# One head of 96 loaded in an order whose outermost count is 8 (softmax times V, one core)

## Chip, core, metric

One core of a Trainium2 chip. The time is what the device takes for one execution, in microseconds (us); lower is better. Quoted times are medians. Ratios are the mean time of one kernel's fast runs over that of the other's fast runs of the same rounds, so they are not quite the ratios of the medians. "More than before" in the experiments is the difference of the two medians of one call. DRAM is the memory off the core that holds the inputs and SBUF the memory on the core with 128 partitions into which loads write.

## The reference

```python
scores: (8, 12, 1024, 1024) float32, v: (8, 12, 1024, 64) float32
attn = np.exp(scores - scores_max)
attn = attn / (np.sum(attn, axis=-1, keepdims=True) + 1e-8)
return np.matmul(attn, v).astype(np.float32)
```

That is 96 heads. Each reads 4 MB of scores and 256 KB of v, and writes 256 KB.

## The kernel before

What matters is how a head is brought in. A head is a tile of 128 partitions; partition p takes 8 adjacent rows of scores, 32 KB in one piece. From here on, a row is such a 32 KB piece. All transfers go through one queue in a fixed order, and the load of head n+4 is asked for when head n is nearly done. (Cuts are marked with `# ...`.)

```python
AHEAD = 4
sc_bh  = scores.rearrange("b h (p r) j -> (b h) p r j", p=P)
v_bh   = v.rearrange("b h (p c) d -> (b h) p c d", p=P)
out_bh = out.rearrange("b h (p r) d -> (b h) p r d", p=P)
# ...
def load(n):
    v_sb = v_pool.tile([P, C, D], FP32, tag="v_sb", name="v_sb")
    queue(nc.sync.dma_start(out=v_sb[:], in_=v_bh[n]))
    s_nat = s_pool.tile([P, R, SK], FP32, tag="s_nat", name="s_nat")
    step = EB if n == BH - 1 else R
    for r in range(0, R, step):
        queue(
            nc.sync.dma_start(out=s_nat[:, r : r + step, :], in_=sc_bh[n, :, r : r + step, :])
        )
    loaded[n] = (s_nat, v_sb)
# ... per head: exp on ACT, transposes on PE, copies on DVE, matmuls with v, then
    if r == R - 1:
        queue(nc.sync.dma_start(out=out_bh[n], in_=st["out_sb"][:]))
# ...
        if r == R - 1 and n + AHEAD < BH:
            load(n + AHEAD)
```

The softmax here doesn't subtract the row's maximum and nothing guards it: scores larger than these inputs give would overflow.

## Time and profile before

| | before |
|---|---|
| time | 1089.68 us |
| one head, from issue to issue | 11.01 us |
| busiest compute engine in 11 us | PE, 8.15 us |
| a 32 KB scores row on one DMA engine, median | 1.216 us |
| transfers of the one queue, share of 16 DMA engines | 98.5% |

Here, in addition, is the page's rate of transfer in 40 equal slices of the span (27 us each), and the rate in two stretches in the middle, in the order stretch, length, busy time of PE, weight loads, DVE, ACT and POOL with their instructions, then clock, DMA share and GB/s.

```profile
GB/s 396 423 430 425 423 423 427 427 426 428 427 422 423 424 431 427 422 426 424 431 425 429 425 426 424 425 429 428 424 423 430 424 426 427 428 420 428 426 398 160
```

```profile
529.00:540.00 11.00, 8.02 (x128) 7.53 (x128) 6.56 (x13) 7.31 (x5) 0.62 (x1) 0.84 1.01 427
540.00:551.00 11.00, 7.87 (x128) 7.49 (x128) 6.55 (x13) 7.30 (x5) 0.62 (x1) 0.83 1.01 427
```

From the second slice to the last but two the rate stays between 420 and 431, and 427 GB/s is about 16 times the 27 GB/s of one engine (32 KB in 1.216 us). Nearly the whole time of the kernel is this one number.

One thing about the sixteen engines is in no view and comes from the trace's completion records, sixteen per load. The completions of one load lie 0.6 us apart at the start of the kernel, 1.9 us at 35 us, and 10.4 us in the middle (for head 47: first 528.25, last 538.63). The engines drift apart until some are nearly a head ahead of others, and by the last full load the spread is 20 us. The trace has a candidate for what drives them apart. Beside the loads it shows packets of 16 KB on a queue of their own (count, MB, share of 16 engines):

```profile
q8 instruction: 96, 1.57, 0.6%
```

They come about once per head and last 1.07 us. Likewise about once per head one engine falls back: the delays of the sixteen behind the first one add up to 1.6 us more with each head (median). That fits, but no run tests it.

The packet records name the queue and not the engine. Where the text below says "all engines", it means that no fast row, or next to none, is left in that stretch.

### The profile page before, as it was taken

The page shows a single profiled execution, that of the slowest core. Times are in us where ns is not written, and L with a number is a line of the kernel's source. Part 1 is how long each engine was busy: PE and PEld are TensorE (multiplying, and loading weights), DVE is VectorE, ACT ScalarE, POOL GpSimd, SP SyncE. Part 2 cuts the span into 40 slices and gives each one's busy share as a digit, 9 for nine tenths or more (in the row PEclk, how much of TensorE's full clock was granted, in tenths as well). Part 3 has the DMA queues.
Part 4 walks back from the last instruction along what each step waited for, and adds up shares of the span by engine and source line. Part 5 has one row for each costly group of instructions (what it writes and reads, how often), then busy time and mean ns, then how long its engine had stood idle before and what let it go on. Part 6 is the DMA issues. An engine that isn't in the chain of part 4 may idle for free.

```text
span 1088.4 us, 27687 instructions
## 1 busy us (share of the span) xinstructions
PE 782.8 (72%) x12288; PEld 743.7 (68%) x12288; DVE 628.2 (58%) x1156; ACT 704.0 (65%) x385; POOL 60.1 (6%) x102
## 2 busy tenths in 40 slices
PE   3767777676777767677776767777676777767676
PEld 3667667676766767677676767677676767767676
DVE  2556556565555655556565655655565565556555
ACT  4667576666757666665766666575665757566675
POOL 0000000000000000000000000000000000000000
PEclk9888878778787877878888887878888787787888
DMA  9999999999999999999999999999999999999994
GB/s 396 423 430 425 423 423 427 427 426 428 427 422 423 424 431 427 422 426 424 431 425 429 425 426 424 425 429 428 424 423 430 424 426 427 428 420 428 426 398 160
DMA packets 42024, 454.77 MB, mean 418 GB/s; under 512 B 4656, under 2 KB 4656, under 8 KB 29232
## 3 DMA queue, kind: packets, MB, share of 16 engines
q1 hardware_dynamic: 41904, 453.00, 98.5%
q8 instruction: 96, 1.57, 0.6%
q14 instruction: 24, 0.20, 0.0%
HBM read 427.82 MB, written 25.17 MB: 416 GB/s over the span
## 4 chain that ended last, share of the span: by engine, by line
DMA 96%; DVE 1%; PE 1%; issue 0%; SPq 0%; ACT 0%; DVEq 0%; ACTq 0%
DMA out_dram<-out_sb 69%; DMA s_nat<-in_scores_dram 18%; DMA v_sb<-in_v_dram 9%; DVE out_sb L89 1%; PE psT L140 1%; PE psO L77 0%; SPq L120 0%; ACT p_nat L136 0%; DVE pt L146 0%; SPq L115 0%; DVE recip L88 0%; DVEq L89 0%; SPq L96 0%; ACTq L136 0%
## 5 line engine op out<-in xcount | busy, mean ns | idle before, releaser
L136 ACT ACTIVATE p_nat<-s_nat 128x2048 f16<-128x2048 f32 x384 | 702.8, 1901 | 375.8 <-DMA s_nat<-in_scores_dram 364.7
L140 PE MATMUL psT<-ident,p_nat 128*128 128x128 f16 x6144 | 621.6, 264 | 274.5 <-ACT p_nat L136 273.5
L140 PEld LDWEIGHTS <-p_nat 128*128 128x128 f16 x6144 | 524.9, 155 | 301.5 <-ACT p_nat L136 295.2
L146 DVE COPY pt<-psT 128x1024 f16<-128x1024 f16 x768 | 529.0, 691 | 307.2 <-PE psT L140 285.4
L77 PE MATMUL psO<-vones,pt 128*128 128x65 f16 x6144 | 343.0, 204 | 27.3 <-DVE pt L146 26.3
L77 PEld LDWEIGHTS <-pt 128*128 128x128 f16 x6144 | 295.4, 107 | 39.2 <-DVE pt L146 38.3
L89 DVE TENSOR_TENSOR out_sb<-psO,recip 128x256 f32<-128x256 f32 x192 | 73.6, 420 | 98.7 <-DMA out_dram<-out_sb 98.6
L130 POOL CAST vones<-v_sb 128x512 f16<-128x512 f32 x96 | 59.4, 619 | 1007.3 <-DMA v_sb<-in_v_dram 995.5
L88 DVE RECIPROCAL recip<-psO 128x4 f32<-128x4 f32 x192 | 34.1, 178 | 49.9 <-PE psO L77 49.9
L136 ACT ACT_TABLE_LOAD x1 | 1.3, 1283 | 0.7 <-PEq L168 0.7
L64 DVE MEMSET vones<- 128x8 f16 x3 | 0.1, 65 | 0.8 <-PEq L168 0.8
L58 DVE CAST ident<-ident 128x128 f16<-128x128 f32 x1 | 0.2, 227 | 0.4 <-POOL ident masks.py:199 0.4
masks.py:199 POOL TENSOR_SCALAR_AFFINE_SELECT ident<-ident 128x128 f32<-128x128 f32 x1 | 0.3, 294 | 0.1
masks.py:197 POOL MEMSET ident<- 128x128 f32 x1 | 0.2, 205 | 0.3 <-POOLq L168 0.3
L168 POOL MEMSET const-float32-0.0<- 128x1 f32 x1 | 0.1, 99 | 0.2 <-issue 0.2
L168 POOL MEMSET const-bfloat16-1.0<- 128x1 bf16 x1 | 0.1, 102 | 0.0
L168 POOL MEMSET const-uint8-127<- 128x1 uint8 x1 | 0.1, 102 | 0.0
L168 POOL MEMSET const-float32-1.0<- 128x1 f32 x1 | 0.1, 99 | 0.0
## 6 DMA issues: line engine op xcount, KB each, us to landing
s_nat<-in_scores_dram SPq DMA_DIRECT2D x95, 4096.0 KB, 32.5
v_sb<-in_v_dram SPq DMA_DIRECT2D x96, 256.0 KB, 23.5
out_dram<-out_sb SPq DMA_DIRECT2D x96, 256.0 KB, 32.4
s_nat<-in_scores_dram SPq DMA_DIRECT2D x4, 1024.0 KB, 23.8
```

What stands on the lines that cost most here:

```text
L58: nc.vector.tensor_copy(out=ident16[:], in_=ident32[:])
L64: nc.vector.memset(vo[:, :, D : D + 1], 1.0)
L77: nc.tensor.matmul(out=psO[:, g, :], lhsT=pt[:, c * P : (c + 1) * P], rhs=st["vones"][:, c, :], start=(c == 0), stop=(c == C - 1),)
L88: nc.vector.reciprocal(out=recip[:], in_=psO[:, :, D : D + 1])
L89: nc.vector.tensor_tensor(out=st["out_sb"][:, r - G + 1 : r + 1, :], in0=psO[:, :, 0:D], in1=recip[:].to_broadcast([P, G, D]), op=mybir.Al ...
L130: nc.gpsimd.tensor_copy(out=vones[:, :, 0:D], in_=v_sb[:])
L136: nc.scalar.activation(out=p_nat[:], in_=s_nat[:, r : r + EB, :], func=EXP)
L140: nc.tensor.transpose(out=psT[:, c * P : (c + 1) * P], in_=p_row[:, c, :], identity=ident16[:],)
L146: nc.vector.tensor_copy(out=pt[:], in_=psT[:])
L168: nc = _bacc.Bacc("TRN2", target_bir_lowering=False, num_devices=1)
```

## The change

The intent is to let eight engines instead of sixteen carry one head in the middle, by giving the load an outermost count of 8. Memory rows then land in permuted partitions, and the output store of that head undoes the permutation.

```diff
         if r == R - 1:
-            queue(nc.sync.dma_start(out=out_bh[n], in_=st["out_sb"][:]))
+            dst = out_bh[n]
+            if n == BH // 2:
+                dst = dst.rearrange("(b a) r d -> a b r d", a=8)
+            queue(nc.sync.dma_start(out=dst, in_=st["out_sb"][:]))
 ...
         step = EB if n == BH - 1 else R
+        if n == BH // 2:
+            queue(
+                nc.sync.dma_start(
+                    out=s_nat[:],
+                    in_=sc_bh[n].rearrange("(b a) r j -> a b r j", a=8),
+                )
+            )
+            loaded[n] = (s_nat, v_sb)
+            return
```

## The prediction

> **What bounds the kernel now.** I first read the page's opening lines, for which engine is full, and then its chain of waits, for what the end hangs on.
>
> ```profile
> PE 782.8 (72%) x12288; PEld 743.7 (68%) x12288; DVE 628.2 (58%) x1156; ACT 704.0 (65%) x385; POOL 60.1 (6%) x102
> DMA  9999999999999999999999999999999999999994
> ...
> q1 hardware_dynamic: 41904, 453.00, 98.5%
> ...
> DMA 96%; DVE 1%; PE 1%; issue 0%; SPq 0%; ACT 0%; DVEq 0%; ACTq 0%
> ```
>
> No compute engine is busy for over 72%. The transfers of one queue take 98.5% of what 16 DMA engines have, in every slice but the last, and 96% of the chain is DMA. The kernel is a stream of heads through the DMA engines. Next I read the issue queue in a quiet stretch, for the rhythm of one head and for how far ahead the kernel asks, and then its waits.
>
> ```profile
> 516.68 0.33 SPq L115 DMA_DIRECT2D v_sb<-in_v_dram  x1
> 517.38 0.33 SPq L120 DMA_DIRECT2D s_nat<-in_scores_dram  x1
> 518.19 0.34 SPq L96 DMA_DIRECT2D out_dram<-out_sb  x1
> 527.69 0.33 SPq L115 DMA_DIRECT2D v_sb<-in_v_dram  x1
> ...
> SPq L115 <- DMA s_nat<-in_scores_dram: 803.6, 89, 10.4
> ...
> s_nat<-in_scores_dram SPq DMA_DIRECT2D x95, 4096.0 KB, 32.5
> ```
>
> One head takes 527.69 - 516.68 = 11.01 us. A scores load lands 32.5 us after its issue, which is three heads. The queue's main wait, in front of the next v load, is for a scores load to land. The built program says which one: there are eight completion semaphores, and each issue waits for the one issued eight before it. Counting v, scores, out, v, ..., the v load of head k waits for the scores of head k-3. So about three heads are in flight, and the four buffers are not the limit.
>
> The trace's packet records give the rate of one engine. A scores row is one packet of 32768 bytes, median 1.216 us, which is 27 GB/s; a v or output row is one of 2048 bytes, 0.084 us. Each of 16 engines has 8 rows of each kind per head: 8 x 1.216 + 16 x 0.084 = 11.07 us, against a period of 11.01. So every engine is full without a gap, and whatever one engine is given in addition has to be paid at the end, unless it is made up by idle time that does not exist. Compute has room:
>
> ```profile
> 513.00:524.00 11.00, 8.15 (x139) 7.77 (x137) 6.58 (x13) 7.31 (x5) 0.62 (x1) 0.84 1.01 427
> ```
>
> The columns are PE, weight loads, DVE, ACT, POOL, clock, DMA share and GB/s: the busiest engine works 8.15 us of 11.00. So compute does not make a late head later; it only moves with it.
>
> [...]
>
> **The change, part by part.** Nothing is added to any compute engine, and the order of instructions on the queue stays the same; the other 95 heads are untouched. The permutation is undone by the output store, so the result is right. What changes is head 48's 128 rows: sixteen per engine on engines 0 to 7, none on 8 to 15.
>
> Step 1, engine time. Engines 0 to 7 carry 8 extra rows of 32 KB: 8 x 1.216 = 9.73 us; and 8 extra output rows: 8 x 0.084 = 0.67 us. Together 10.4 us.
>
> Step 2, who pays. [...]all later heads are again split evenly over 16. Engines 0 to 7 are full before and after, so they never make up the 10.4 us; the other eight run ahead and idle later. Head 48 lands on the loaded eight 1.3 + 19.5 = 20.8 us after head 47 (v and out first). Until then the others have heads 49 and 50 in their rings, 2 x 11.0 + 1.3 = 23.3 us of work, so they don't even run dry. This step alone makes 1089.7 + 10.4 = 1100.1 us.
>
> Step 3, [...]Engines are not in step, though. The 2 KB packets around one head start between about 503.0 and 507.5 us[...]. When head 48 takes over 23 us, engines 8 to 15 run dry because the issue of head 51 waits for head 48; that idle time is the lead they have anyway, and costs nothing more.
>
> [...]0.55 x 31 + 0.2 x 20 + 0.25 x 10.4 = 24 us. As the middle of the distribution lies on the strong side, I say 26: 1089.7 + 26 = 1116 us.
>
> **Rivals.** (a) Engine time alone, 1100 us: speaks for it that 27 GB/s is seen as an engine's rate[...].[...] (b) It hides: engines 8 to 15 run ahead, head 48 is late but something absorbs it, about 1090 us. For it: compute has 2.8 us of room per head, and three heads are in flight. Against: the full engines are DMA's own, and depth moves no work from one engine to another. I give it 0.04. (c) The late head starves compute, and compute becomes the bound behind it. PE needs 8.15 us per head and gets 11, so each wait is recovered within the next heads; adds nothing. (d) The DRAM side is read in steps of 256 KB[...] and is slower for it; the trace has no such pattern, and I can't size it, but it only adds.
>
> **Range and chances.** Rival (a) sets the lower edge, 1099; the strong form without much skew the upper one, 1131. The line at 2% is 1111.5 us, which the strong form passes and (a) does not: slower 0.56, same 0.43, faster 0.01.
>
> **What would show it.** If step 1 and 2 hold, all of the loss is between the landing of head 47 and of head 48 (about 530 to 590 us), and the heads after that follow at 11.0 us again. If step 3 holds, the packets of 32 KB in that stretch last 2.4 to 3.6 us instead of 1.216, on even the engines that don't carry head 48, and the DMA rate falls below 400 GB/s there while engines are busy. [...]It is wrong altogether if the load is still split over 16 (no change), or if engines differ between load and store (0.7 us less).

The sum. The grounds of step 3, a model of where each engine writes and of how engines slow each other there, are cut. In its strong form, step 1's 10.4 us included, it came to 28 to 33 us more than before. The sum weighs three cases: the strong form as 31 us with 0.55, a weaker one as 20 us with 0.2, and step 1 alone, 10.4 us, with 0.25. It came to 24 us, raised to 26, so 1116 us. Only 10.4 was worked out from the trace before; what 31 and 20 are made of, no trace showed then. The sign against step 3: all packets at 1.22 us, head 48 about 21 us after head 47, and 427 GB/s until the end. The 2.4 to 3.6 us for step 3 are two and three times 1.216, an estimate of the model.

The engines. "Engines 0 to 7" and "8 to 15" are names for the eight that carry head 48 and the eight that don't; no record numbers them. The trace after bears the number out: the changed load has eight engine completions where a plain load has sixteen, and the page counts 4640 packets under 512 B against 4656 before (16 for each of the 291 transfers), eight fewer for the load and eight for the store.

The waits. That an issue waits for the one eight before it is in the trace before: the landings name eight semaphores, and the v load issued at 538.69 us follows the landing, at 538.63, of the scores load issued at 506.37, eight issues earlier.

## The result, and the profile after

1128.4 us (four runs, 1125.91 to 1129.83) against 1089.68: ratio 1.0352, 95% interval 1.0331 to 1.0373, slower. The time lies in the predicted range, 12 us above the predicted 1116. The profiled run is the fastest of the four; its span is 1124.1 us against 1088.4, so the profile has 35.7 of the 38.7 us to show.

The page's rate of transfer after, 28 us to a slice:

```profile
GB/s 401 424 425 423 428 423 428 426 424 426 426 427 425 425 426 426 426 424 404 214 260 407 429 404 423 427 423 430 422 427 426 427 421 425 424 428 424 424 388 90
```

Two slices at about half the rate, and a last one of 90 in place of 160. The rest is as before. The stretches of the middle, same columns as above:

```profile
511.00:522.00 11.00, 7.85 (x128) 7.48 (x125) 6.55 (x12) 7.31 (x5) 0.62 (x1) 0.78 1.01 424
529.00:540.00 11.00, 8.01 (x128) 7.62 (x128) 5.71 (x10) 5.56 (x4) 0.19 (x1) 0.84 1.08 248
540.00:551.00 11.00, 2.43 (x22) 2.31 (x23) 1.91 (x4) 4.39 (x3) 0.62 (x1) 0.55 1.01 223
551.00:562.00 11.00, 6.62 (x109) 6.37 (x106) 4.65 (x9) 2.93 (x2) 0.00 (x0) 0.81 1.01 215
562.00:573.00 11.00, 0.00 (x0) 0.00 (x0) 0.00 (x0) 0.00 (x0) 0.00 (x0) 0.50 1.07 229
573.00:584.00 11.00, 0.00 (x0) 0.00 (x0) 0.00 (x0) 0.00 (x0) 0.00 (x0) 0.50 0.77 245
584.00:595.00 11.00, 7.05 (x101) 6.93 (x102) 5.37 (x10) 7.32 (x4) 0.62 (x1) 0.62 0.91 378
```

Read the last two columns together. From 529 to 573 the DMA share is 1.0, all sixteen engines have a packet in flight all the time, and yet they move 215 to 248 GB/s instead of 427. So this is not idle engines: every engine is slow. The packet records say the same: between 531 and 576 us the kernel before has 516 rows of 32 KB, 513 of them under 1.3 us; the kernel after has 267, and not one under 2.2 us (median 2.47). As no fast row is left, the engines that carry nothing of head 48 are among the slow ones. Only between 573 and 584 are some engines idle as well (0.77).

The issue queue and its longest wait, and ACT (start, length, what, and in brackets how long ACT had been idle and for what):

```profile
516.89 0.79 SPq L123 DMA_DIRECT2D s_nat<-in_scores_dram  x1
546.57 0.33 SPq L118 DMA_DIRECT2D v_sb<-in_v_dram  x1
585.94 0.33 SPq L118 DMA_DIRECT2D v_sb<-in_v_dram  x1
596.55 0.33 SPq L118 DMA_DIRECT2D v_sb<-in_v_dram  x1
```

```profile
SPq L118 <- DMA s_nat<-in_scores_dram: 828.8, 89, 37.1
```

```profile
546.61 7.32 ACT L148 ACTIVATE p_nat<-s_nat 128x2048 f16<-128x2048 f32 x4 [12.04 <-DMA s_nat<-in_scores_dram]
585.99 7.32 ACT L148 ACTIVATE p_nat<-s_nat 128x2048 f16<-128x2048 f32 x4 [32.06 <-DMA s_nat<-in_scores_dram]
596.59 7.32 ACT L148 ACTIVATE p_nat<-s_nat 128x2048 f16<-128x2048 f32 x4 [3.29 <-PE psO L77]
```

The line with L123 is the changed load. Head 47, issued before it and unchanged, lands at 546.5 instead of 538.6. Head 48 lands at 585.9, 39.4 us after head 47. From then on heads come every 11 us or so again, and ACT has its usual 3 to 5 us of rest per head. Next to nothing is recovered later (by the completions, head 48 lands 36.2 us later than before, heads 50 and 51 35.3 us later), and nothing more is lost in compute.

Where the time went, worked out from the rates: from 529 to 584 the mean rate is 232, so 55 x (1 - 232/427) = 25 us are lost there. In the 22 us after that (378, then 388) it is 2 us. Over the kernel's last 47 us some 2.5 MB fewer are moved than before, because most of the engines are through with their work: 6 us. (Of the sixteen completions of the last load, twelve lie within 0.3 us and the last one comes 17.7 us after the first.) That makes 33 of 35.7; the rest I did not place.

### The profile page after: what moved, and what is told of

The parts are those of the page before. It is cut to its first block, busy times and chain, and to the rows that moved or that the text cites. A ratio compares the mean times of both kernels' runs of the same rounds, so it can differ in the third digit from the quotient of the medians.

```text
span 1124.1 us, 27687 instructions
## 1 busy us (share of the span) xinstructions
PE 786.7 (70%) x12288; PEld 748.4 (67%) x12288; DVE 627.3 (56%) x1156; ACT 704.0 (63%) x385; POOL 59.9 (5%) x102
## 2 busy tenths in 40 slices
DMA packets 42008, 454.77 MB, mean 405 GB/s; under 512 B 4640, under 2 KB 4640, under 8 KB 29216
## 4 chain that ended last, share of the span: by engine, by line
DMA 92%; another core or an unknown queue 2%; PE 2%; DVE 2%; issue 1%; ACT 1%; SPq 0%; DVEq 0%; ACTq 0%
DMA out_dram<-out_sb 61%; DMA s_nat<-in_scores_dram 22%; DMA v_sb<-in_v_dram 9%; PE psT L152 2%; DVE out_sb L89 1%; PE psO L77 1%; ACT p_nat L148 1%; DVE pt L158 0%; DVE recip L88 0%; SPq L132 0%; SPq L118 0%; DVEq L89 0%; ACTq L148 0%; SPq L99 0%
## 5 line engine op out<-in xcount | busy, mean ns | idle before, releaser
L77 PEld LDWEIGHTS <-pt 128*128 128x128 f16 x6144 | 298.6, 107 | 39.1 <-DVE pt L158 38.2
```

What stands on the lines that cost most here:

```text
L77: nc.tensor.matmul(out=psO[:, g, :], lhsT=pt[:, c * P : (c + 1) * P], rhs=st["vones"][:, c, :], start=(c == 0), stop=(c == C - 1),)
```

## The experiments

Twelve kernels. The record's verdicts go by a line at 2%: it calls outer16, halves64, extra_own, early16, one_engine and two_engines "same" and extra_other "unclear". For each of them the 95% interval of the ratio lies above 1 all the same, and the text goes by that. The last column is from the packet records, as a median or a range of the text below; fences of stretches have the columns given above.

| kernel | time | more than before | rows of 32 KB in the affected stretch |
|---|---|---|---|
| the change | 1128.40 | 38.7 | all 16 engines, 2.47 us |
| all_k8 | 2382.74 | | 2.48 us at first, 1.22 us later |
| outer16 | 1108.10 | 18.2 | all 16 engines, 2.48 us |
| halves64 | 1108.16 | 18.2 | all 16 engines, 2.50 us |
| near8 | 1126.05 | 36.1 | all 16 engines, 2.47 us |
| extra_own | 1095.76 | 5.8 | 1.22 us |
| extra_other | 1113.56 | 23.6 | all 16 engines, 2.53 us |
| outer2 | 1171.42 | 81.5 | mixed |
| early8 | 1137.39 | 47.5 | all 16 engines, 3.67 us |
| early16 | 1100.33 | 10.4 | all 16 engines, 2.58 us |
| one_engine | 1101.73 | 11.8 | 277 of 295 under 1.3 us, 8 over 2.2 |
| two_engines | 1104.32 | 14.5 | most of them, 2.37 us |
| v16all | 1195.80 | 105.9 | 1.30 us from 500 to 600 us |

The theory at the start was the prediction's step 3. What can be tested of it here is this: how fast an engine writes depends on which partitions it and the others write at the time. Below it is called the place theory, and two engines that slow each other in this way are said to meet. The rivals were: eight engines beside eight others are slow in themselves ("pairing"), and the order in DRAM is slow. In the expectations a number that follows a cut and has no theory named before it is the place theory's, and its 2.4 us a row (twice 1.216) is an estimate.

The number of engines of a load was read, where a page was printed, from its packets under 512 B, 4656 or sixteen per transfer before: all_k8 has 3136 (eight for each of 190 transfers), outer16 4656 (sixteen), near8 4648 (eight for the load), extra_own 4672 (eight for each added load), early8 4640 (eight for load and store), outer2 4628 (two for load and store), two_engines 4658 (two for the added load). For halves64, extra_other, early16, one_engine and v16all it was not counted.

### all_k8: every head on eight engines

```diff
+        if n < BH - 1:
+            queue(nc.sync.dma_start(out=s_nat[:], in_=sc_bh[n].rearrange("(b a) r j -> a b r j", a=8)))
+            loaded[n] = (s_nat, v_sb)
+            return
```
(and the output store likewise)

> All heads but the last are loaded and stored with outer count 8, so engines 8 to 15 carry only v. [...]rows of 32 KB last about 2.4 us though the other eight engines carry no scores, some 40 us per head, 3.6 to 3.9 ms. Pairing theory (a loaded engine is halved only because one of the other eight works beside it): rows last 1.22 us, 20.9 us per head, about 2.0 ms.

Measured 2382.74 us, between the two, and the page shows why. Its rates, 60 us to a slice, and two stretches:

```profile
GB/s 117 115 122 127 130 139 142 167 172 196 212 210 210 213 205 206 212 205 200 212 208 215 214 209 210 212 208 214 214 207 210 213 211 214 215 210 198 207 212 128
```

```profile
20.00:120.00 100.00, 16.63 (x256) 15.89 (x256) 12.93 (x24) 14.64 (x8) 1.24 (x2) 0.73 0.50 112
1200.00:1300.00 100.00, 41.32 (x640) 39.47 (x640) 32.23 (x59) 34.72 (x20) 3.09 (x5) 0.67 0.52 212
```

The DMA share is 0.5 in both: eight engines are at work. At first they move half of what eight engines can, 2.48 us a row, with nobody beside them but the small v loads. Pairing cannot do that; loaded engines that meet can. Later the same eight run at 212 GB/s, 1.22 us a row. The completion records show what differs: around 120 us the eight finish a load within 1.1 us of each other, around 1200 us within 25 us, a whole head. That fits engines that meet while they are in step and hardly meet once they have drifted apart. That the drift is the cause is not shown by itself, and the run is a single one.

### outer16: the same order with count 16

```diff
+                in_=sc_bh[n].rearrange("(b a) r j -> a b r j", a=16)
```
(for head 48, load and store)

> Head 48 with outer count 16: all 16 engines carry 8 rows each as before[...]. [...]5 to 10 us more than before, 1095 to 1100 us. Pairing and DRAM-order theories: no engine has more than before, 1090 us.

18.2 us more (ratio 1.0167, 1.0152 to 1.0182), though no engine has a row more than before. Its rate in two stretches:

```profile
529.00:540.00 11.00, 8.04 (x128) 7.66 (x128) 5.80 (x11) 5.97 (x4) 0.59 (x1) 0.84 1.06 236
540.00:551.00 11.00, 1.93 (x18) 1.80 (x18) 1.45 (x3) 3.89 (x3) 0.62 (x1) 0.57 1.02 232
```

Engine time and pairing predicted nothing here. What is left is where the engines write (halves64 takes away the permutation as well). But the cost is about twice what I gave for it, which the early runs take up.

### halves64: two plain loads of 64 partitions

```diff
+            for h in (0, 64):
+                queue(nc.sync.dma_start(out=s_nat[h : h + 64], in_=sc_bh[n, h : h + 64]))
```

> Head 48 as two plain loads of 64 partitions, 16 engines each (4 rows per engine and load). [...]rows last 2.4 us, head 48 takes 19.5 instead of 9.7 us: about 1099 us. Theory that only engine time counts: 1090 us, rows 1.22 us.

18.2 us more again (1.0169, 1.0153 to 1.0184). A stretch of it:

```profile
540.00:551.00 11.00, 2.42 (x22) 2.30 (x23) 1.90 (x4) 4.38 (x3) 0.62 (x1) 0.51 1.01 219
```

No permutation and plain rows in order, and the same slow rows (2.50 us) at a DMA share of 1.01. What changed is that each load writes 64 partitions and not 128.

### near8: the other side's order

```diff
+            rows = scores.rearrange("b h (p r) j -> (b h p) r j", p=P)
+            near = rows[n * P : n * P + 8 * 17].rearrange("(a b) r j -> a b r j", a=8)
+            queue(nc.sync.dma_start(out=s_nat[:], in_=near[:, 0:16]))
```

> Wrong on purpose (head 48 reads rows 17a+b)[...]. [...]the DRAM order does not matter, 1128 us as with the change (0.7 less, as the output store is plain). DRAM-order theory: rows back to 1.22 us, about 1100 us.

By the edit, the load reads eight blocks of 16 adjacent rows, 17 rows (544 KB) apart, into the same tile with the same count of 8. 1126.05 us (1125.04 to 1128.38), wrong result. Against the change's 1125.91 to 1129.83 it is 2.6 us less in the medians over before; 0.7 was expected of the plain store, and the ranges overlap. Its rate in the stretch where the change has 223:

```profile
540.00:551.00 11.00, 1.77 (x16) 1.68 (x16) 1.42 (x3) 3.74 (x3) 0.62 (x1) 0.60 1.04 229
```

So the order of the DRAM rows is not the cause.

### extra_own and extra_other: the same added loads to two places

```diff
+            extra = x_pool.tile([P, 6144], FP32, tag="extra", name="extra")
+            flat = sc_bh[n].rearrange("p r j -> p (r j)")
+            for h in (0, 32):
+                part = flat[h : h + 32, 0:6144].rearrange("(b a) x -> a b x", a=8)
+                queue(nc.sync.dma_start(out=extra[B + h : B + h + 32], in_=part))
```
(head 48's own load is unchanged; B = 0 in extra_own, 64 in extra_other)

> Head 48 is loaded as before. Two added loads on engines 0 to 7 (outer count 8, 32 partitions each, 24 KB rows, to partitions 0 to 63 of a tile nobody reads)[...]. 8 rows x 0.91 us = 7.3 us more for eight engines. If the engine's own time binds (steps 1 and 2 of the prediction): 1097 us, rows stay at 1.22 us. If eight engines beside eight others are slow in themselves[...]: 1110 us or more.

> The same added loads, same engines, bytes and DRAM rows, but to partitions 64 to 127[...]. [...]8 rows x 1.82 = 14.6 us more, 1104 us, and rows of 1.22 us remain beside rows of 2.4. [...]the landing of one head is spread over 10.4 us between engines, so the halved stretch is about 2 x 10.4 + 14.6 = 35 us, 25 us more: 1112 to 1115 us.

(Both forms in extra_other's expectation are the place theory's: in the first only engines that meet are slowed, in the second all are halved while any two meet.)

This is the pair that decides. Same bytes, rows and order; only the partitions written differ. 5.8 us more (1.0037 to 1.0067) against 23.6 (1.0199 to 1.0230). First extra_own, then extra_other:

```profile
540.00:550.00 10.00, 8.81 (x128) 8.44 (x128) 5.81 (x10) 5.63 (x4) 0.24 (x1) 0.71 1.01 429
```

```profile
540.00:550.00 10.00, 0.85 (x8) 0.85 (x9) 0.76 (x2) 2.82 (x2) 0.62 (x1) 0.51 1.00 222
```

Into partitions 0 to 63, eight engines carry a surplus at full rate (429 GB/s), and it costs 5.8 of the 7.3 us that it takes them; what takes up the other 1.5 us no run shows. Into partitions 64 to 127, all sixteen halve (222 GB/s), as the second form in the expectation has it: from 531 to 556 us no row is under 2.1 us, though the engines of one load are spread over some 10 us (10.4 in the trace before). The number fits as well, 1113.6 in 1112 to 1115.

### outer2: two engines carry the head

```diff
+                in_=sc_bh[n].rearrange("(b a) r j -> a b r j", a=2)
```
(for head 48, load and store)

> Head 48 with outer count 2: two engines carry 64 rows each. Engine time alone: 56 x 1.216 + 56 x 0.084 = 73 us more, 1163 us. [...]If only those that meet are slowed: most rows elsewhere stay at 1.22 us, about 1175 us. If all are halved[...]: nearly all rows 2.4 us as long as the fourteen have work (some 40 us), about 1185 us.

1171.42 us (two runs), and both theories are half wrong. Between 530 and 537 us only one of the two engines seems to be at head 48: 65 of 72 rows last about 1.22 us, and the starts and ends of the slow ones join into two chains, as of two engines. Between 543 and 546, when the second has come to it, no row is under 2.1 us. From 594 to 603, with fresh heads for the other fourteen, all 54 rows are slow. So "all are halved" falls in that form; the last two experiments test it alone.

### early8 and early16: the same at head 2, where the engines are in step

```diff
-        if n == BH // 2:
+        if n == 2:
```
(early8; early16 the same with the count 16)

> The change at head 2 in place of head 48. Early in the before kernel the sixteen completions of one load lie within 0.6 to 1.9 us of each other, in the middle 10.4 us. If the lost time is the halved stretch from the first engine's entry to the last one's exit, it is shorter here: 2 x 1.9 + 16 x 2.43 - 1.9 - 9.7 = 31 us, plus 0.7: 1121 us. If the spread does not matter: 1128 us as in the middle.

> Outer count 16 at head 2, where the engines are in step, in place of head 48. [...]every row of head 2 lasts 2.43 us on all engines and the halved stretch is 8 rows long: 9.7 us more, and about 1 us for the spread: 1100 to 1102 us. If the spread of the engines had no part in the 18 us that this order cost at head 48: 1108 us.

early8 goes against me: 47.5 us more (1.0433, 1.0415 to 1.0450), not 31. A stretch of it:

```profile
40.00:50.00 10.00, 0.00 (x0) 0.00 (x0) 0.00 (x0) 0.00 (x0) 0.00 (x0) 0.50 1.01 146
```

All 236 rows between 25 and 78 us last 3.37 to 3.72 us, median 3.67: three times 1.22, on all engines, and 146 is about a third of 427. Sixteen rows of 3.67 us instead of eight of 1.22 are 49 us. The expectation had reckoned with twice, 2.43 us; why it is three times no run shows. early16 is as expected, its rows at 2.58 us: 10.4 us more (1.0077 to 1.0111), one head at half rate, and 7.8 us less than the same order costs in the middle:

```profile
30.00:40.00 10.00, 4.78 (x89) 4.53 (x87) 4.39 (x9) 1.38 (x1) 0.00 (x0) 0.84 1.00 208
```

So for the count 16 the spread of the engines seems to make it dearer: they come to the odd head one after the other over 10 us, and the halved stretch starts with about the first and ends with about the last. For the count 8 the spread seems to make it cheaper, by 9 us: of the 267 slow rows of the change only 3 are over 2.7 us, so the threefold pace is next to never reached. Head 2 differs from head 48 in more than the spread (it is in the kernel's start), so this reading is a fit and not shown.

### one_engine and two_engines

```diff
+            queue(nc.sync.dma_start(out=extra[64:81], in_=flat[0:17, 0:6144]))
```
(two_engines: 34 partitions, `extra[64:98]` and `flat[0:34, 0:6144]`)

> One added load of 17 partitions (64 to 80, 24 KB rows, to a tile nobody reads), beside an unchanged head 48: [...]one engine carries it, 15.5 us alone[...]. If one meeting slows all: rows of all engines 2.4 us for some 31 us, 1112 to 1122 us. If only the two that meet are slowed: most rows stay at 1.22 us in that stretch, and the time is set by the one engine's delay less its lead: 1105 to 1121 us, so the rows decide, not the time.

> As the one-engine load, with 34 partitions (64 to 97): [...]two engines carry 17 rows of 24 KB each[...]. If meetings stay local also when there are two: most rows at 1.22 us, about 1102 us as with one engine. If two meetings are enough to halve all sixteen, as the last part of the outer-count-2 run suggests: rows of 2.4 us on all engines while both are at it, 1108 to 1122 us.

First one_engine (11.8 us more), then two_engines (14.5 us more), each with two runs:

```profile
529.00:540.00 11.00, 8.08 (x128) 7.63 (x128) 6.49 (x13) 7.25 (x5) 0.62 (x1) 0.84 1.03 403
540.00:551.00 11.00, 9.07 (x128) 8.70 (x128) 5.99 (x11) 6.08 (x4) 0.62 (x1) 0.69 1.00 397
```

```profile
529.00:540.00 11.00, 8.02 (x128) 7.53 (x128) 5.80 (x10) 5.88 (x4) 0.50 (x1) 0.84 1.05 269
540.00:551.00 11.00, 3.91 (x46) 3.79 (x47) 2.83 (x5) 5.88 (x4) 0.62 (x1) 0.53 1.02 251
```

One load into partitions 64 to 80, expected on one engine, goes at about half its pace and slows few others: between 530 and 558 us, 277 of 295 other rows stay under 1.3 us, 8 are over 2.2, its own 24 KB rows last mostly 1.65 to 1.94 us (0.91 in extra_own), and the rate is 400. With two engines on partitions 64 to 97, 125 of 164 rows are over 2.2 us in the same stretch, and 11 under 1.3. Here the step from local to general lies between these two loads. In time the difference is small; with one engine it is probably its own delay that sets the end (17 rows of some 1.8 us), which no run separates.

### v16all: short meetings in every head

```diff
-        queue(nc.sync.dma_start(out=v_sb[:], in_=v_bh[n]))
+        queue(nc.sync.dma_start(out=v_sb[:], in_=v_bh[n].rearrange("(b a) c d -> a b c d", a=16)))
```

> Wrong on purpose: every v load (256 KB, 2 KB rows) with outer count 16, scores and output unchanged. [...]If even such short meetings halve everything, most of the time is halved: over 1400 us. If short ones are taken up by what the engines hold, at most 0.7 us per head more: 1090 to 1157 us.

105.9 us more, 1.1 us per head. Its output is wrong, which doesn't matter for the time. Neither bound of the expectation holds: it is over the 0.7 us per head of v's own rows (8 x 0.084 us on each engine) and far below general halving. Between 500 and 600 us scores rows last 1.30 us in the median, none over 1.9. Over the whole run their mean is 1.35 us against 1.22 before, and 8 x 0.13 = 1.04 us per head is nearly all of the 1.1. Short loads in the other order thus slow many rows somewhat, all along the run, and go unseen if one looks for rows at half speed.

## Why the prediction was right, and where its size was off

**What bounds the kernel**: right. All of the loss is a loss of DMA rate, and compute follows.

**How many engines**: right, eight; the changed load has eight engine completions in the trace (567.9 to 585.9 us) where all other loads have sixteen. Which partitions each engine takes is in no record.

**Step 1, engine time, 10.4 us**: shown alone by extra_own, at 5.8 of 7.3 us. It is a real term. In the change it is mostly not a term of its own, though: the loaded engines' sixteen rows are all slow, and it is within that product.

**Step 2, who pays**: that later heads make up nothing is right; the heads follow at 11 us again, and the final slice is at 90 GB/s, most of the engines being done. That the other eight don't run dry did not hold: the share of 0.77 between 573 and 584 shows that some do, as step 3 said they would when head 48 takes over 23 us (it took 39.4).

**Step 3, where the engines write**: that this is the cause is right (extra_own against extra_other, 5.8 against 23.6 us, with near8 ruling out DRAM order and outer16 ruling out engine time). How engines slow each other there was an assumption; no run shows the mechanism, and the size was off. It gave 28 to 33 us, and the whole is 38.7. Two terms were mis-sized, and in opposite directions:

- The rows of head 48 were given too much. In the terms some rows were to go at a third of full speed and others at half. In fact nearly all rows go at one pace, half speed, on loaded engines and others: 16 x 2.47 = 39.5 us. By the completions head 48 lands 39.4 us after head 47 instead of 11.0, so this term is 28.4 us where step 3 with step 1 had about 33.
- Head 47 was given nothing. The lead of the engines was read as some 4 us from the 2 KB packets, and only taken off. The packets of neighbouring heads cannot be told apart there, and the lead is 10.4 us by the completions. It has a cost that the sum lacked: the engines that come last still have most of head 47 to carry when the first ones start on head 48, and they are halved from then on. Head 47 lands at 546.5 instead of 538.6, 7.9 us late.

28.4 + 7.9 + 0.7 for the output rows is 37.0, against 35.7 for this profiled run and 38.7 in the medians. That the strong form's 33 came near is in part luck, as the two errors partly cancel.

**The average over rivals** took another 5 us off: the strong form alone, at 31, would have been 1121. (The three shares sum to 1 already, so the 0.04 for rival (b) stands outside them.) Rival (a) had 0.25: in the trace before, 513 of 516 rows between 531 and 576 us take under 1.3 us, and nothing in it spoke for step 3.

**Rivals**: (a), engine time alone, falls with outer16 (18.2 us without an extra row on any engine). (b), hidden, falls with the result. (c), compute as a second bound, falls with ACT's 3.29 us of rest right after the late head. (d), DRAM order, falls with near8.

What stays open: what the engines share when they slow each other, and why one_engine slows next to no row but its own (8 of 295 others over 2.2 us) while two_engines slows most (125 of 164). No run here shows it.

## What to carry to other kernels

In a kernel bound by DMA like this one, keep all 128 partitions as one outermost dimension on both sides of a large load. Loading a head with an outer count of 8 (215 to 248 GB/s), with one of 16 (222 to 236) or as two loads of 64 partitions (207 to 242) halved the rate of all sixteen engines here, from 427, for as long as several of them were at it (one_engine's load left it at 397 to 403), and no count of engines or bytes shows that beforehand. To tell slow engines from idle ones, read the DMA share beside the GB/s: a share of 1.01 at 223 GB/s meant here that the packets themselves were slow (2.47 us a row). And when engines run freely for long, look at the completions of one transfer before assuming that they are in step.
